# Routed experts in two-lane steps of 64 rows, in plain fp32, with rows added to the tokens by the transfers

## The chip, the cores and the metric

The kernel runs on one core of one Trainium2 chip. The metric is the device time of one execution in microseconds (us). Runs of the kernel before took 1578.53, 1578.96 and 1581.05 us, a median of 1578.96.

## What is computed

One layer of a decoder trunk for 1024 tokens of width 1024. The first half (a mixer of a convolution, a state-space branch and attention) is not touched. The second half is a mixture of experts with a layer norm behind it:

```
e_idx, e_w = grouped_top2_route(h2d, router_w, router_bias)      # 2 of 32 experts for each token
y = routed_experts(h2d, e_idx, e_w, w1, w3, w2)                  # (silu(x w1) * (x w3)) w2, by expert
y = y + swiglu(h2d, shared_w1, shared_w3, shared_w2)             # one shared expert
x = layer_norm(ALPHA * x + g2 * y, ln_g, ln_b)                   # ALPHA = 2 ** 0.25
```

1024 tokens with two experts each are 2048 rows, sorted by expert. An expert's weights are three pieces of 1 MB (1024 x 512 for the two up-projections side by side, in two pieces, and 256 x 1024 for the down-projection). With these inputs 23 of the 32 experts get rows.

## The kernel before

Rows of one expert are cut into blocks of 128 (BLK). There are 33 blocks here, and the loop's first stretch (STRETCH, line 42) runs 33 without asking. For each block `block` (line 1676) writes out the order of TensorE, ScalarE, VectorE and GpSimd by hand:

- `fetch` and `fetch_w` (from line 1595) load the weights of the block after next on SP's queue, each load under a condition that skips it if the expert in that buffer is already the right one. `ex_w` splits each weight piece into a rounded high half (ScalarE, line 125) and the rest (VectorE, line 129), both in the fp32r format.
- `ex_x` transposes the gathered 128 rows (8 transposes of 128 columns, line 1635), splits them in the same way, and `gather` (line 1610) has GpSimd issue an indirect transfer for the rows of block b + 2.
- `ex_up` multiplies with `mm3`: each product of 128 x 512 is three fp32r matmuls (lines 140 to 142). 8 products are the two up-projections.
- `ex_mid` transposes the hidden rows of block b - 1 (line 1654) and splits them; `ex_down` makes 4 products for that block, scales each row by its routing weight on ScalarE (line 1671), and GpSimd scatters the rows by an indirect transfer (line 1672) into `yd`. `yd` holds 2 x 1024 rows, one for each token and choice. Empty rows of a block have an index outside of the bounds and are left out.

A block so issues 36 matmuls of 512 columns and 10 transposes. The work of `ex_mid` and `ex_down` for a block stands one block later.

Ahead of the loop `shared_down` (line 1528) computes base = ALPHA * x + the shared expert (already times g2) for eight tiles of 128 tokens and keeps them in SBUF. `exp_start` (line 1562) issues the first conditional loads.

Behind the loop `final` (line 1706) loads g2 and the norm's two rows, spreads them over the partitions by matmuls (line 1719), loads both rows of each token (line 1729), adds them (for six of eight tiles by identity matmuls in plain fp32, line 1741), multiplies by g2, adds the base, and takes the layer norm: sum on VectorE, sum of squares on ScalarE (line 1753), scale and shift on ScalarE, GpSimd (line 1781) or VectorE (lines 1783, 1798), and the store on SP's queue (line 1784).

Another stage that the prediction reads is the state-space branch: at line 1013 it multiplies with tiles of 128 x 64, two side by side in TensorE's columns.

Of the kernel before, what the change touches and what calls it, by code (L numbers as in the profile page):

```python
# [39 lines left out]
SLOTS = {"wa": ["h2", "l2", "h3", "l3", 0, "x0"], "wb": [1, "h0", "l0", "h1", "l1", "x1"]}  # L40
PROLOGUE = ((0,), (0, 0), (0,), (0, 1), (0, 2), (0, 3), (1, 0), (0, 4))
STRETCH = (0, 33, 35, 39, MAXB)
# [38 lines left out]
class K:  # L81
# [86 lines left out]
    def build(self):  # L168
        with ExitStack() as ctx:
# [13 lines left out]
            self.x1d, self.h2d, self.yd = dt("x1d", [S, D]), dt("h2d", [S, D]), dt("yd", [2 * S, D])  # L183
# [33 lines left out]
            if self.stop in ("post", "shared"):  # L217
                return
            with ExitStack() as st:
                self.banks_for(tr=2, th=1, h=2, y=3)  # L220
                self.experts(pool(st, "exq"))
            est.close()
            with ExitStack() as st:
                self.banks_for(y=8)
                self.final(pool(st, "fin"))
# [12 lines left out]
    def pair(self, n, dt=F32R):  # L238


        if str(n)[0] == "x":
            return self.exp.tile([128, 2, D], dt, name=n, tag=n)
# [1146 lines left out]
    def ffn(self, wst):  # L1389
# [23 lines left out]
        self.wraw = [[self.pair(2 + 3 * z + q, F32) for q in range(3)] for z in range(2)]  # L1413
        for z in range(2):
            for q in range(3):
                nc.sync.dma_start(out=self.wraw[z][q][:].rearrange("p k n -> p (k n)"), in_=a["exp"][FIRST[z], q])
# [5 lines left out]
        with tc.manual_schedule(engines={mybir.EngineType.DVE}):  # L1422
            self.logits(P, 3)
            self.shared_up(w, hs, 0, 0)
            R.pick(6, 8)
            self.shared_up(w, hs, 0, 1)
            next(rows)
            self.shared_up(w, hs, 1, 0)
            self.shared_up(w, hs, 1, 1)
            g2 = self.shared_down(P, hs, rows)  # L1430
        wst.close()
        if self.stop == "shared":
# [3 lines left out]
            for i in range(NT):  # L1436
                self.dump(f"base{i}", self.base[i][:])
            return
        self.g2 = g2
# [88 lines left out]
    def shared_down(self, P, hs, rows):  # L1528
        nc, a = self.nc, self.a
        v = nc.vector  # L1530
        g2 = self.row_bc(P, "g2", self.adad[3:4, :])
# [12 lines left out]
        self.base = []  # L1544
        for i in range(NT):
            base = self.bslot(i)
            nc.sync.dma_start(out=base[:], in_=self.x1d[i * 128:(i + 1) * 128, :])
            self.base.append(base)
# [10 lines left out]
            self.ex_w(*PROLOGUE[i])  # L1559
        return g2  # L1560

    def exp_start(self):

        nc = self.nc
        self.turn = {"wa": 0, "wb": 0}
        self.ew, self.ex, self.eh = {}, {}, {}
        self.last_load = None
        self.nb = nc.values_load(self.be[0:1, 2 * MAXB:2 * MAXB + 1], min_val=0, max_val=MAXB)
# [5 lines left out]
    def experts(self, P):  # L1574
        tc, nc = self.tc, self.nc
# [6 lines left out]
        with ExitStack() as arms:  # L1582
            for b0, b1 in zip(STRETCH, STRETCH[1:]):
                if b0:
                    arms.enter_context(tc.If(self.nb > b0))
                    self.last_load = None
                with tc.manual_schedule(engines=MANUAL | {mybir.EngineType.Pool}):
                    self.ex_w(b0, 0)
                    self.ex_x(b0, 0)
                    self.ex_x(b0, 1)  # L1590
                    self.ex_w(b0, 1, 2, 3, 4)
# [3 lines left out]
    def fetch(self, b):  # L1595

        with ExitStack() as st:
            if self.last_load is not None:
                st.enter_context(self.tc.issue_after(self.last_load))
            self.fetch_reg(b)  # L1600
            for q in range(2):
                self.fetch_w(b, q)

    def fetch_reg(self, b):
        sync = self.nc.sync
        self.reg = (sync.value_load(self.be[0:1, b:b + 1], min_val=0, max_val=E - 1),
                    sync.value_load(self.be[0:1, MAXB + b:MAXB + b + 1], min_val=0, max_val=1))

# [5 lines left out]
    def fetch_w(self, b, q):  # L1614
        e, ld = self.reg
        d = self.nc.sync.dma_start(out=self.wraw[b % 2][q][:].rearrange("p k n -> p (k n)"), cond=ld,
                                   in_=self.a["exp"][bass.ds(e, 1), q].rearrange("z p n -> (z p) n"))
        self.last_load = d.ins

    def ex_w(self, b, *qs):  # L1620

        for q in qs:
            if (b, q) in self.ew:
                continue
            tg = "wa" if q < 4 else "wb"
            w = self.ew[b, q] = self.pair(SLOTS[tg][self.turn[tg] % len(SLOTS[tg])])
            self.turn[tg] += 1
            self.split_into(w[:, 0], w[:, 1], self.wraw[b % 2][q // 2][:, q % 2])

    def ex_x(self, b, n):  # L1630

        x = self.ex[b, n] = [self.exp.tile([128, 512], F32R, name="x" + z, tag="x" + z, bufs=2) for z in "hl"]
# [4 lines left out]
        self.split_into(x[0][:], x[1][:], ps[:])  # L1637
        if n and b + 2 < MAXB:
            self.gather(b + 2)

    def ex_up(self, b, ps, n):

        xh, xl = self.ex.pop((b, n))
        for k in range(4 * n, 4 * n + 4):
            w = self.ew[b, k // 2]
            xs, ws = slice((k % 4) * 128, (k % 4) * 128 + 128), slice((k % 2) * 512, (k % 2) * 512 + 512)
            self.mm3(ps[:], xh[:, xs], xl[:, xs], w[:, 0, ws], w[:, 1, ws], k == 0, k == KT - 1)

    def ex_mid(self, b):
# [5 lines left out]
        self.eh[b] = [self.exp.tile([128, 256], F32R, name="h" + z, tag="h" + z, bufs=1) for z in "hl"]  # L1655
        self.split_into(self.eh[b][0][:], self.eh[b][1][:], pt[:, :256])

    def ex_down(self, b):

        nc, P = self.nc, self.exp  # L1660
        hh, hl = self.eh.pop(b)
        w = [self.ew.pop((b, q)) for q in (4, 5)]
        y = P.tile([128, D], F32, name="y", tag="y", bufs=2)
        ps = [self.ps("y") for _ in range(2)]
        for k in range(2):
            ks = slice(k * 128, (k + 1) * 128)
            for n in range(2):
                sl = slice(n * 512, (n + 1) * 512)
                self.mm3(ps[n][:], hh[:, ks], hl[:, ks], w[k][:, 0, sl], w[k][:, 1, sl], k == 0, k == 1)
        for n in range(2):  # L1670
            nc.scalar.activation(out=y[:, n * 512:(n + 1) * 512], in_=ps[n][:], func=AF.Copy, scale=self.roww[:, b:b + 1])  # L1671
        nc.gpsimd.indirect_dma_start(out=self.yd[:], in_=y[:], in_offset=None,  # L1672
                                     out_offset=bass.IndirectOffsetOnAxis(ap=self.idx[:, 1, b:b + 1], axis=0),
                                     bounds_check=2 * S - 1, oob_is_err=False)

    def block(self, b, first, last):

        v, act = self.nc.vector, self.nc.scalar
        if b + 2 < MAXB:
            self.fetch(b + 2)  # L1680
        self.ex_w(b, 5)
        if b + 2 < MAXB:
            self.fetch_w(b + 2, 2)
        ps = self.ps("h")
        self.ex_up(b, ps, 0)
        if not first:
            self.ex_mid(b - 1)
        if not last:
            self.ex_w(b + 1, 0)
            self.ex_x(b + 1, 0)  # L1690
        self.ex_up(b, ps, 1)
        if not last:
            self.ex_x(b + 1, 1)
            self.ex_w(b + 1, 1, 2)
# [3 lines left out]
        if not last:  # L1698
            self.ex_w(b + 1, 3, 4)
        if not first:  # L1700
            self.ex_down(b - 1)
        if last:
            self.ex_mid(b)
            self.ex_down(b)

    def final(self, P):

        nc = self.nc
        v, act, gp, pe = nc.vector, nc.scalar, nc.gpsimd, nc.tensor
        ys = []  # L1710

        row = P.tile([128, 3, D], F32, name="frow")
# [391 lines left out]
```

## Time and profile before

| | |
|---|---|
| median of the timed runs | 1578.96 us |
| the profiled execution | 1582.0 us |
| its span, first to last instruction | 1579.9 us |
| TensorE busy | 1419.6 us (90%) |
| VectorE busy | 1196.8 us (76%) |
| ScalarE busy | 733.4 us (46%) |
| GpSimd busy | 442.5 us (28%) |
| mean granted clock of TensorE | 0.954 |
| moved by the DMA engines | 247.50 MB |

Everything in the trace is timed from the start of the span. In the trace PE is TensorE's matmuls, PEld its weight loads, DVE VectorE, ACT ScalarE, POOL GpSimd and SP the engine that issues most transfers. L1672 is line 1672 of the kernel. A matmul record's duration includes its way through the array, so the pitch of neighbouring records, not their duration, is what one costs. An indirect transfer on POOL shows the time that POOL takes to issue it; the chain of work and the waits tell when it landed.

### The profile page before, as it was taken

Reading aid. Unit: us, or ns where it says so; the run is one execution under the profiler, and the core shown is the slowest. Engines: PE = TensorE matmul, PEld = TensorE weight load, DVE = VectorE, ACT = ScalarE, POOL = GpSimd, SP = SyncE. Lnnn points to the kernel's source line nnn. Section 1 sums busy time; section 2 is a strip of 40 time slices with the busy share of each in tenths; the row PEclk is TensorE's granted clock in tenths of the full one; section 3 lists DMA queues with packets and bytes.
Section 4 is the critical chain, followed back from the end, with each engine's and each line's share of the span. In section 5 each row is a group of like instructions: output and inputs, shape, how many; then the busy total and the mean of one; then the engine's idle time right before and its main releaser. Section 6 shows DMA issues by size and latency. Waiting matters only on the chain.

```text
span 1579.9 us, 20183 instructions
## 1 busy us (share of the span) xinstructions
PE 1419.6 (90%) x6996; PEld 1144.4 (72%) x6996; DVE 1196.8 (76%) x1861; ACT 733.4 (46%) x1192; POOL 442.5 (28%) x599
## 2 busy tenths in 40 slices
PE   5599799479999999999799979999979999999983
PEld 3477678368888887887588867788967888888841
DVE  8464687898775547756587788778887999999948
ACT  6232112242223334130477763335424998999853
POOL 7999930000000000006211252400322322222216
PEclk9799999799999999999799998999999999999977
DMA  9232221132122248968200035634623777777643
GB/s 382 80 113 88 73 58 27 67 101 97 56 107 107 107 145 308 326 161 224 36 15 12 4 114 192 225 133 151 251 79 115 303 282 287 289 297 272 255 182 146
DMA packets 79940, 247.50 MB, mean 157 GB/s; under 512 B 18460, under 2 KB 29780, under 8 KB 71000
## 3 DMA queue, kind: packets, MB, share of 16 engines
q1 hardware_dynamic: 53670, 200.47, 36.0%
q10 hardware_dynamic: 15218, 24.68, 4.5%
q0 software_dynamic: 10944, 20.99, 4.2%
q8 instruction: 56, 0.92, 0.2%
q14 instruction: 52, 0.43, 0.1%
HBM read 252.74 MB, written 55.10 MB: 195 GB/s over the span
## 4 chain that ended last, share of the span: by engine, by line
PE 58%; DVE 14%; POOL 12%; DMA 7%; issue 5%; ACT 3%; ACTq 0%; DVEq 0%; POOLq 0%; SPq 0%
PE ps_mm L140 9%; PE ps_mm L141 9%; PE ps_mm L142 9%; DMA yd<-y,idx 4%; PE ps_up L140 3%; PE ps_h L140 3%; PE ps_h L142 3%; PE ps_h L141 3%; PE ps_up L141 3%; PE ps_up L142 3%; PE ps_O L1272 2%; PE ps_T L1258 2%; PE ps_y L140 1%; PE ps_y L142 1%; PE ps_tr L1635 1%
## 5 line engine op out<-in xcount | busy, mean ns | idle before, releaser
L1138 POOL TENSOR_TENSOR mg<-mg,sg 128x512 f32<-128x512 f32 x16 | 23.5, 1476 | 496.4 <-DVE sg L1137 492.8
L140 PE MATMUL ps_mm<-hh,wlo 128*128 128x512 f32 x304 | 123.5, 406 | 22.7 <-ACT sg L1075 15.6
L142 PE MATMUL ps_mm<-hh,whi 128*128 128x512 f32 x304 | 123.1, 405 | 0.0
L141 PE MATMUL ps_mm<-hl,whi 128*128 128x512 f32 x304 | 122.7, 404 | 0.0
L125 ACT CAST whi<-raw 128x1024 fp32r<-128x1024 f32 (+1 forms) x45 | 46.8, 1040 | 134.0 <-PE ps_up L142 65.2
L1672 POOL DMA_INDIRECT yd<-y,idx x33 | 46.5, 1409 | 170.4 <-ACT y L1671 98.4
L140 PEld LDWEIGHTS ps_mm<-hh,wlo 128*128 128x128 f32 x304 | 58.7, 193 | 37.6 <-ACT sg L1075 16.1
L129 DVE TENSOR_TENSOR qh<-wo,qh 128x1024 fp32r<-128x1024 f32 x66 | 80.5, 1220 | 5.1 <-ACT qh L125 5.1
L129 DVE TENSOR_TENSOR ql<-wo,ql 128x1024 fp32r<-128x1024 f32 x66 | 79.5, 1219 | 4.8 <-ACT ql L125 4.8
L129 DVE TENSOR_TENSOR wlo<-raw,whi 128x1024 fp32r<-128x1024 f32 x44 | 60.4, 1373 | 26.5 <-ACT whi L125 26.5
L125 ACT CAST qh<-wo 128x1024 fp32r<-128x1024 f32 x66 | 70.0, 1061 | 4.1 <-DMA wo<-exp 4.1
L142 PEld LDWEIGHTS ps_mm<-hh,whi 128*128 128x128 f32 x304 | 58.6, 193 | 14.9 <-issue 1.0
L141 PEld LDWEIGHTS ps_mm<-hl,whi 128*128 128x128 f32 x304 | 58.8, 193 | 13.7 <-issue 0.2
L125 ACT CAST ql<-wo 128x1024 fp32r<-128x1024 f32 x66 | 68.2, 1052 | 0.0
L125 ACT CAST xh<-ps_tr 128x512 fp32r<-128x512 f32 x66 | 39.5, 599 | 55.5 <-PE ps_tr L1635 55.4
L1610 POOL DMA_INDIRECT xg<-h2d,idx x35 | 37.1, 1061 | 77.1 <-PE ps_tr L1635 63.5
L1244 DVE TENSOR_REDUCE sm<-ps_S 128x1 f32<-128x256 f32 (+3 forms) x64 | 49.2, 770 | 10.8 <-PE ps_S L1241 10.1
L129 DVE TENSOR_TENSOR pl<-ps_T,ph 128x512 fp32r<-128x512 f32 (+1 forms) x80 | 45.9, 581 | 14.0 <-ACT ph L125 12.6
L140 PE MATMUL ps_up<-ah,wlo 128*128 128x512 f32 x128 | 50.6, 403 | 5.1 <-ACT ah L125 2.9
L391 DVE TENSOR_TENSOR sp<-ps_mm,sp 128x512 f32<-128x512 f32 x48 | 32.8, 686 | 28.0 <-PE ps_mm L142 27.8
L1245 ACT ACTIVATE p<-ps_S,sm 128x256 f32<-128x256 f32 (+3 forms) x64 | 48.5, 758 | 10.0 <-DVE sm L1244 9.4
L140 PE MATMUL ps_mm<-wo,ml 128*128 128x512 f32 x128 | 50.0, 398 | 2.8 <-DVE sg L1354 2.8
(727 smaller groups left out, 4733.2 us busy)
## 6 DMA issues: line engine op xcount, KB each, us to landing
wo<-exp SPq DMA_DIRECT2D x111, 1024.0 KB
raw<-w_in SPq DMA_DIRECT2D x43, 512.0 KB
adr<-w_ada SPq DMA_DIRECT2D x32, 512.0 KB
wada<-w_ada SPq DMA_DIRECT2D x16, 512.0 KB
fy<-yd SPq DMA_DIRECT2D x16, 512.0 KB
sga<-sg ACTq DMA_DIRECT2D x8, 512.0 KB
sgc<-sg ACTq DMA_DIRECT2D x8, 512.0 KB
sgs<-sg ACTq DMA_DIRECT2D x8, 512.0 KB
```

Of the source, the lines that this page charges most:

```text
L125: nc.scalar.copy(out=hi, in_=src)
L129: e.tensor_tensor(out=lo, in0=src, in1=hi.bitcast(F32), op=ALU.subtract)
L140: mm(ps, wl, xh, start=first, stop=False)
L141: mm(ps, wh, xl, start=False, stop=False)
L142: mm(ps, wh, xh, start=False, stop=last)
L391: v.tensor_tensor(out=out, in0=p, in1=x, op=op)
L1244: v.tensor_reduce(out=sm[:], in_=x, axis=AX.XY if two else AX.X, op=ALU.max, negate=True)
L1245: act.activation(out=y, in_=x, func=AF.Exp, bias=sm[:], accum_out=d)
L1258: pe.transpose(pt[:, k2 * 256 + qi * 128:k2 * 256 + qi * 128 + 128], prob[h, c, qi][:, ks], self.ident[:])
L1272: pe.matmul(po[:, 0:256], vv[:, kt, h].rearrange("p z d -> p (z d)"), x[z], start=kt == 0 and z == 0, stop=kt == 2 * c + 1 and z == 1)
L1610: self.nc.gpsimd.indirect_dma_start(out=self.xg[b % 2][:], out_offset=None, in_=self.h2d[:], in_offset=bass.IndirectOffsetOnAxis(ap=self.i ...
L1672: nc.gpsimd.indirect_dma_start(out=self.yd[:], in_=y[:], in_offset=None, out_offset=bass.IndirectOffsetOnAxis(ap=self.idx[:, 1, b:b + 1], ...
```

## The change

Blocks hold 64 rows. Two blocks are worked on at once, as a step: the first in lane 0 (columns 0 to 63 of TensorE, partitions 0 to 63 of the result), the second in lane 1 (64 to 127). Blocks are dealt to steps so that the lanes have their own experts, and each lane has its own two sets of raw weight buffers. 47 blocks of these inputs make 24 steps, and the loop's first stretch is now 24 steps. The weights, rows and hidden rows are used as plain fp32; there are no splits in the loop. The gated and weighted rows are added to `yd`, which now holds one row for each token and starts as the base, by two indirect transfers for each step, one a lane. The last norm reads one row for each token, and runs on ScalarE and VectorE alone.

```diff
-BLK = 128
+BLK = 64
+MAXS = (MAXB + 1) // 2
-STRETCH = (0, 33, 35, 39, MAXB)
+SLOTS = ((2, 3, 4), ("h2", "l2", "h3")), ((5, 6, 7), ("l3", 0, 1))
+STRETCH = (0, 24, 25, 27, MAXS)
...
+            nc.scalar.dma_start(out=self.yd[i * 128:(i + 1) * 128, :], in_=base[:])
...
     def fetch_w(self, b, q):
+            for z in range(2):
+                e, ld = self.regs[b][z]
+                d = self.nc.sync.dma_start(out=self.wx[z, b % 2][q][:].rearrange("p k n -> p (k n)"), cond=ld,
+                                           in_=self.a["exp"][bass.ds(e, 1), q].rearrange("z p n -> (z p) n"))
...
     def ex_x(self, b, n):
-        self.split_into(x[0][:], x[1][:], ps[:])
+        self.nc.scalar.copy(out=self.ex[b][:, n * 512:(n + 1) * 512], in_=ps[:])
+    def mm2(self, ps, x, w, first, last):
+        for z in range(2):
+            self.nc.tensor.matmul(ps[z * 64:(z + 1) * 64, :], x[:, z * 64:(z + 1) * 64], w[z], start=first, stop=last,
+                                  tile_position=(0, 64 * z))
     def ex_up(self, b, ps, n):
         for k in range(4 * n, 4 * n + 4):
+            self.mm2(ps, self.ex[b][:, k * 128:(k + 1) * 128],
+                     [self.wx[z, b % 2][k // 4][:, k // 2 % 2, ws] for z in range(2)], k == 0, k == KT - 1)
     def ex_mid(self, b):
+        self.nc.vector.tensor_copy(out=self.eh[b][:], in_=pt[:, :256])
     def ex_down(self, b):
         y = P.tile([128, D], F32, name="y", tag="y", bufs=2)
+        for n in range(2):
+            ps, sl = self.ps("y"), slice(n * 512, (n + 1) * 512)
+            for k in range(2):
+                self.mm2(ps, ht[:, k * 128:(k + 1) * 128], [self.wx[z, b % 2][2][:, k, sl] for z in range(2)], k == 0, k == 1)
+            nc.vector.scalar_tensor_tensor(out=y[:, sl], in0=ps[:], scalar=self.roww[:, b:b + 1], in1=self.g2[:, sl],
+                                           op0=ALU.mult, op1=ALU.mult)
+        for z in range(2):
+            nc.gpsimd.indirect_dma_start(out=self.yd[:], in_=y[:], in_offset=None,
+                                         out_offset=bass.IndirectOffsetOnAxis(ap=self.idx[:, 1 + z, b:b + 1], axis=0),
+                                         bounds_check=S - 1, oob_is_err=False, compute_op=ALU.add)
     def block(self, b, first, last):
         self.ex_up(b, ps, 0)
+            self.fetch_reg(b + 2)
+            self.fetch_w(b + 2, 0)
             self.ex_mid(b - 1)
             self.ex_x(b + 1, 0)
         self.ex_up(b, ps, 1)
+            self.fetch_w(b + 2, 1)
             self.ex_x(b + 1, 1)
             self.ex_down(b - 1)
+                self.fetch_w(b + 1, 2)
...
     def final(self, P):
+            nc.sync.dma_start(out=r[i][:], in_=self.yd[i * 128:(i + 1) * 128, :])
+        def stats(i):
+            act.activation(out=junk[:], in_=r[i][:], func=AF.Identity, accum_out=c(0, i))
+            act.mul(out=c(2, i), in_=c(0, i), mul=-1.0 / D)
+            act.activation(out=junk[:], in_=r[i][:], func=AF.Square, bias=c(2, i), accum_out=c(3, i))
+            act.activation(out=c(3, i), in_=c(3, i), func=AF.Identity, scale=1.0 / D, bias=eps[:])
             act.activation(out=c(4, i), in_=c(3, i), func=AF.Sqrt)
         def norm(i):
+            v.scalar_tensor_tensor(out=r[i][:], in0=r[i][:], scalar=c(2, i), in1=self.lg[:], op0=ALU.add, op1=ALU.mult)
...
+            v.scalar_tensor_tensor(out=r[i][:], in0=r[i][:], scalar=c(4, i), in1=self.lb[:], op0=ALU.mult, op1=ALU.add)
+            nc.sync.dma_start(out=self.out[i * 128:(i + 1) * 128, :], in_=r[i][:])
```

The transposes stay full-width (128 x 128). The router's index work is changed to blocks of 64 and to an index list for each lane; the two rows of the last norm are loaded ahead of the loop on ScalarE's queue (`last_rows`).

## Rows read from the trace of the kernel before

**Rows 1.** Busy time by stretch: us, busy (x instructions) by engine, clock, DMA share, GB/s.
```profile
1165.00:1204.00 39.00, 30.20 (x154) 24.16 (x152) 32.98 (x60) 8.32 (x10) 12.36 (x8) 0.91 0.14 46
1204.00:1516.00 312.00, 308.62 (x1510) 254.84 (x1510) 285.01 (x324) 273.67 (x389) 79.27 (x65) 1.00 0.71 264
1516.00:1580.00 64.00, 33.69 (x60) 13.71 (x60) 45.71 (x69) 27.33 (x61) 30.27 (x11) 0.71 0.50 199
```

**Rows 2.** The chain that ended last, from 1100: start us, us, what.
```profile
1204.14 0.50 PE ps_h L140
...
1402.87 0.44 PE ps_tr L1635 x4
...
1412.21 0.44 PE ps_tr L1635 x4
...
1440.59 8.06 DMA yd<-y,idx
...
1522.44 4.39 DMA fy<-yd
```

**Rows 3.** Timeline of PE in the last norm: start us, us, what.
```profile
1537.64 14.32 PE L1741 MATMUL ps_y<-fy,ident 128*128 128x512 f32 x33
```

**Rows 4.** Timeline of PE in the state-space stage.
```profile
130.59 0.33 PE L982 MATMUL ps_ss<-ident,kt 128*128 128x128 f32 x1
130.84 1.75 PE L1013 MATMUL ps_ss<-U,W 128*64 128x128 f32 x28
```

**Rows 5.** Groups from 1140 on, by form: busy us, mean ns | idle before, releasers.
```profile
L1672 POOL DMA_INDIRECT yd<-y,idx x33 | 46.5, 1409 | 170.4 <-ACT y L1671 98.4 <-ACT hh L125 36.8 <-ACT qh L125 16.8
...
L125 ACT CAST xh<-ps_tr 128x512 fp32r<-128x512 f32 x66 | 39.5, 599 | 55.5 <-PE ps_tr L1635 55.4
L1610 POOL DMA_INDIRECT xg<-h2d,idx x35 | 37.1, 1061 | 77.1 <-PE ps_tr L1635 63.5 <-DVE hl L129 7.8 <-issue 5.8
...
L1555 DVE SCALAR_TENSOR_TENSOR b<-b,ps_mm 128x512 f32<-128x512 f32 x16 | 10.3, 678 | 0.8 <-PE ps_mm L142 0.8
```

**Rows 6.** Waits of POOL from 1190 to 1519: us in total, times, longest us.
```profile
POOL yd L1672 <- ACT y L1671: 98.4, 21, 4.8
```

**Rows 7.** Stretches cut at landings of scatters in the chain; the last one alone.
```profile
1431.94:1435.95 4.01, 4.01 (x22) 3.31 (x21) 3.92 (x5) 3.14 (x6) 2.03 (x2) 1.00 0.29 111
1440.59:1448.65 8.06, 8.06 (x38) 6.61 (x38) 7.60 (x10) 7.20 (x11) 2.33 (x2) 1.00 0.95 368
1459.23:1465.98 6.75, 6.75 (x33) 5.53 (x33) 6.29 (x8) 5.89 (x9) 2.33 (x2) 1.00 0.96 364
...
1487.18:1496.26 9.08, 9.08 (x47) 7.54 (x46) 8.61 (x11) 8.21 (x13) 2.34 (x2) 1.00 0.96 356
1516.71:1520.00 3.29, 0.00 (x0) 0.00 (x0) 0.06 (x1) 1.00 (x1) 0.98 (x1) 0.90 0.15 47
```

**Rows 8.** Timeline of POOL at the loop's end: [idle before, releaser].
```profile
1497.04 1.00 POOL L1672 DMA_INDIRECT yd<-y,idx  x1 [5.37 <-DMA yd<-y,idx]
...
1516.71 0.98 POOL L1672 DMA_INDIRECT yd<-y,idx  x1 [3.53 <-ACT y L1671]
```

**Rows 9.** Timeline of SP's queue behind the loop.
```profile
1522.04 13.96 SPq L1729 DMA_DIRECT2D fy<-yd  x16
```

**Rows 10.** Groups of the last norm, from 1521, by form.
```profile
L1741 PE MATMUL ps_y<-fy,ident 128*128 128x512 f32 x48 | 23.1, 646 | 0.9 <-DMA fy<-yd 0.9
...
L1753 ACT ACTIVATE junk<-fy,fst 128x1024 bf16<-128x1024 f32 x8 | 9.2, 1148 | 5.5 <-DVE fst L1749 5.3
...
L1783 DVE SCALAR_TENSOR_TENSOR fy<-fy,fst,lb 128x1024 f32<-128x1024 f32 x3 | 3.8, 1278 | 0.0
...
L1759 ACT ACTIVATE fst<-fst,feps 128x1 f32<-128x1 f32 x6 | 1.7, 286 | 0.1
L1760 ACT ACTIVATE fst<-fst 128x1 f32<-128x1 f32 x8 | 1.6, 196 | 2.9 <-DVE fst L1757 2.9
L1753 ACT ACTIVATION_READ_ACCUMULATOR junk<-fy,fst 128x1 f32 x8 | 1.5, 186 | 0.0
```

More of the change, by code (lines that the diff above doesn't have):

```diff
@@ L1614, in fetch_w @@
     def fetch_w(self, b, q):
[L1615 to L1628, printed above, removed]
+        with ExitStack() as st:
+            if self.last_load is not None:
+                st.enter_context(self.tc.issue_after(self.last_load))
+            for z in range(2):
+                e, ld = self.regs[b][z]
+                d = self.nc.sync.dma_start(out=self.wx[z, b % 2][q][:].rearrange("p k n -> p (k n)"), cond=ld,
+                                           in_=self.a["exp"][bass.ds(e, 1), q].rearrange("z p n -> (z p) n"))
+                self.last_load = d.ins
     def ex_x(self, b, n):
-        x = self.ex[b, n] = [self.exp.tile([128, 512], F32R, name="x" + z, tag="x" + z, bufs=2) for z in "hl"]
+        if n == 0:
+            self.ex[b] = self.exp.tile([128, D], F32, name="xt", tag="xt", bufs=2)
         ps = self.ps("tr")
@@ L1662, in ex_down @@
[L1662 removed]
+        ht = self.eh.pop(b)
         y = P.tile([128, D], F32, name="y", tag="y", bufs=2)
[L1664 to L1669, printed above, removed]
[L1670 to L1671 removed]
@@ L1704, in block, with last_rows @@
             self.ex_down(b)
+            if b + 2 < MAXS:
+                self.fetch_w(b + 2, 2)
+    def last_rows(self, P):
+        self.lg, self.lb = (P.tile([128, D], F32, name=n) for n in ("lg2", "lb2"))
+        for t, n in ((self.lg, "ln_g"), (self.lb, "ln_b")):
+            self.nc.scalar.dma_start(out=t[:], in_=self.a[n][1:2, :].partition_broadcast(128))
     def final(self, P):
         nc = self.nc
-        v, act, gp, pe = nc.vector, nc.scalar, nc.gpsimd, nc.tensor
-        ys = []
-        row = P.tile([128, 3, D], F32, name="frow")
-        for i, src in enumerate((self.adad[3:4, :], self.a["ln_g"][1:2, :], self.a["ln_b"][1:2, :])):
-            nc.sync.dma_start(out=row[0:1, i], in_=src)
-        g2, lg, lb = (P.tile([128, D], F32, name=n) for n in ("g2", "lg2", "lb2"))
-        for i, t in enumerate((g2, lg, lb)):
-            for n in range(2):
-                ps, sl = self.ps("y"), slice(n * 512, (n + 1) * 512)
-                pe.matmul(ps[:], self.ones[0:1, :], row[0:1, i, sl], start=True, stop=True)
-                act.copy(out=t[:, sl], in_=ps[:])
+        v, act = nc.vector, nc.scalar
         st = P.tile([128, 6, NT], F32, name="fst")
@@ L1777, in affine @@
-        def affine(i):
-            r = ys[i][0]
-            if i < LAST:
-                for e, row, op in zip(GL[i], (lg, lb), (ALU.mult, ALU.add)):
-                    (v if e == "v" else gp).tensor_tensor(out=r[:], in0=r[:], in1=row[:], op=op)
-            else:
-                v.scalar_tensor_tensor(out=r[:], in0=ys[i][1][:], scalar=c(4, i), in1=lb[:], op0=ALU.mult, op1=ALU.add)
-            nc.sync.dma_start(out=self.out[i * 128:(i + 1) * 128, :], in_=r[:])
-        GL = ('gg', 'gg', 'gg', 'gg', 'gg', 'vv', 'vv', 'vv')
@@ L1787, in final @@
-        LAST = LT
-        with ExitStack():
-            for j in range(NT + 2):
-                if j < NT:
-                    gated(j, 0)
-                    gated(j, 1)
-                if 0 < j < NT:
-                    root(j - 1)
-                if j < NT:
-                    total(j)
-                    if j >= LAST:
-                        v.scalar_tensor_tensor(out=ys[j][1][:], in0=ys[j][0][:], scalar=c(2, j), in1=lg[:], op0=ALU.add, op1=ALU.mult)
-                    if j == NT - 1:
-                        norm(j - 1)
-                        affine(j - 1)
-                        affine(j - 2)
-                        root(j)
-                        norm(j)
-                        affine(j)
-                        break
-                if j:
-                    norm(j - 1)
-                if j > 1:
-                    affine(j - 2)
+            v.tensor_tensor(out=c(4, i), in0=c(4, i), in1=c(5, i), op=ALU.mult)
@@ L1813 @@
+            v.scalar_tensor_tensor(out=r[i][:], in0=r[i][:], scalar=c(4, i), in1=self.lb[:], op0=ALU.mult, op1=ALU.add)
+            nc.sync.dma_start(out=self.out[i * 128:(i + 1) * 128, :], in_=r[i][:])
+        for i in range(NT + 1):
+            if i < NT:
+                stats(i)
+            if i:
+                norm(i - 1)
 class Route:
```

224 lines of the change are left out of this document (87 added, 137 removed).

## The prediction, made before the changed kernel was run

> **What bounds the kernel now.** I read the stretches first, then the chain of work that ended last, then single timelines. The stretches say what fills the part that changes: from 1204 to 1516 PE is busy 308.62 of 312.00 us at full granted clock, and VectorE (285.01) and ScalarE (273.67) run nearly as full beside it because they make the high and low halves of every weight [rows 1]. So this stretch, the loop over 33 blocks, is TensorE's: it waits for almost nothing. The same view shows PE at 33.69 of 64.00 us after 1516, where the last layer norm runs. The chain's entries give the loop's beat: the first up-projection starts at 1204.14, and the transposes of two neighbouring blocks start at 1402.87 and 1412.21, 9.34 us apart [rows 2]. 33 x 9.34 = 308.2 us, to 1512.3; the last scatter is issued at 1516.71 [rows 8] and landed 3.29 later, at 1520.0 [rows 7], 7.7 us after the loop.
>
> **TensorE after.** The inputs fix the routing: 2048 rows over 23 experts make 47 blocks of 64, so 24 steps, which is also the first stretch that runs unconditionally. A step issues 12 products over both lanes (8 up, 4 down) and 10 transposes. The trace has no 64-column fp32 product of 512, so I bound it. A full-width plain fp32 product: 33 records in 14.32 us, 0.434 each [rows 3], and two records to a product (the stage's 24 products show as 48 [rows 10]), so 0.868. If the two lanes run side by side a pair costs 0.868 too; if one after the other, 1.736. The nearest row is the state-space stage, which already uses 128x64 tiles: 28 records of 128 columns in 1.75 us [rows 4]. One after the other, a 128-column record at 0.109 (a quarter of 0.434) would give 28 x 0.109 = 3.05; side by side 14 x 0.109 = 1.53 and some lead and drain. So they share. The same rows price a change of tile shape: from 130.59 to 130.84 a full-width record takes 0.25 instead of 0.11, about 0.15 lost. A step changes four times between lanes and full-width transposes.
> Step: 12 x 0.868 = 10.4, transposes 10 x 0.11 (four in 0.44 [rows 2]) = 1.1, switches 4 x 0.15 = 0.6: 12.1 us, with bounds 11.4 (no switch cost) and 12.9 (switches at twice that, and a little waiting for the copies). 24 x 12.1 = 290 against 308.2: 18 us less.
> The Trainium skill, "TensorEngine Tiling (Array Packing)", section "Key Properties", says that changing the tiling mode drains TensorE. The trace agrees, with those 0.15 us; by the rule alone no figure follows.
>
> **Splits and evacuations.** All splits go. VectorE keeps two gated evacuations of y (0.678 each, priced by the same operation from PSUM in line 1555), the gate product and the copy of the transposed hidden rows (half a copy's 512 columns, about 0.4 each); ScalarE two copies of x (0.599) and a Silu (about 0.4) [rows 5]. That is 2.2 and 1.6 us of 12.1: both are off the path at no cost, and TensorE covers them. POOL's own part of a step is a gather (1.06) and two scatters (1.41 each) [rows 5], 3.9.
>
> **The adds: the new wait.** Before, a block's scatter starts when its y is ready: what POOL mostly waits for there is ACT's y, 98.4 us in 21 waits [rows 6]. The landing of the one before is what the scatter at 1497.04 waited for, 5.37 us [rows 8]. All scatters write one tensor, so each waits for the last one's landing. Now there are two to a step, and gathers stand behind them on POOL; the y buffers (two) and so VectorE's evacuation and TensorE's third y bank hang on them. With a landing time L and 0.75 from a landing to the next issue (landed at 1496.26 where a stretch of [rows 7] ends, issued at 1497.04 [rows 8]) a step can't be shorter than 2 x (L + 0.75).
> L is in the stretches cut at the landings that the chain names (its entry of 8.06 us [rows 2] is one of these): 3.29 alone, 4.01 at 111 GB/s, and 8.06, 6.75 and 9.08 at 356 to 368 GB/s [rows 7]. So L goes with what else is moving: 4.01 x 111 = 0.45 MB moved meanwhile, 6.75 x 364 = 2.46, 8.06 x 368 = 2.97, 9.08 x 356 = 3.23. Before, an expert's three loads of 1 MB are issued nearly together; now the three stand after up0, up1 and down, some 4 us apart, so about 1.0 MB and the scatter's own quarter meet a scatter. On the line between 0.45 MB and 2.46 MB, 1.25 MB gives 5.1. An add must also read the target. No row shows it: its bounds are nothing, and the part after POOL's issue in the landing alone once more, 3.29 - 0.98 = 2.3 [rows 7, 8]. I take 0.4, near the lower end, because a scatter now carries at most 64 rows and 43 on the average (2048 / 48) where blocks of before held 62 (2048 / 33). L = 5.5, and the floor is 2 x 6.25 = 12.5: a hair above TensorE's 12.1. Taken for all 24 steps the loop is 300 us, to 1504. From both sides: L = 3.3 leaves TensorE's 290; L = 9.08 gives 19.7 a step, 472.
> The routing gives 20 experts to load in the loop (21 before, over 33 blocks), 60 pieces of 1 MB: an expert, 3 MB, in 12.5 us is 240 GB/s, under the 264 that [rows 1] show. Steps with two (three of 24) need 6 MB, 16 us at 370 GB/s; buffers two steps deep absorb it, up to 3 x 4 = 12 us if they don't.
> Ahead of the loop, the six 1 MB loads of step 1 and the base rows' writes to yd are issued in the shared expert's stage, 46 GB/s and a DMA share of 0.14 [rows 1]: at no cost. If the last base's write were late, the first add waits, two steps later; TensorE doesn't. The writes and the two rows of the last norm are issued on ScalarE's queue: a write waits for its base (VectorE's line 1555), and the loop's first copies of x stand behind it, so the loop can't start before the last base; before, it started after that stage too. SP's queue holds in the loop only register reads and loads, each behind the product that frees its buffer, in the order of the steps; a late one holds up only later loads.
>
> **Tail and last norm.** After the loop the last hidden rows, their down product and y take 5 us, and four scatters stand one after the other instead of one: the pair of step 22 (2 x 4.0 alone) while y of 23 is made, then two more (2 x 4.0). 16 us from the loop's end to the last landing against 7.7: +8.3. Landed: 1504 + 16 = 1520, as before.
> Then the norm: first load issued 2.0 after the landing (1522.04 [rows 9] against 1520.0), 4.39 to data as the chain has it before [rows 2]. ScalarE per tile: two passes of 1.148 + 0.186, two small ones of 0.196 and one of 0.286 [rows 10] = 3.35, eight tiles 26.8. VectorE: two passes of 1.278 and about 0.7 of small ones, 3.3, beside it; after the last root 2.0 remain, and a store, taken like that first load, 4.4. Sum 2.0 + 4.4 + 26.8 + 2.0 + 4.4 = 39.6 against 1579.9 - 1520.0 = 59.9 now: -20.3. The 33.69 us of PE, POOL's passes and half of the loads go. Bounds 36 to 44: tile statistics could stall on VectorE's chain.
>
> **Sum.** 1579.9 - 8.2 (loop at 12.5) + 8.3 (tail) - 20.3 = 1559.7 in span. The profiled execution took 1582.0 as a whole, and its span is 0.9 above the median of the timed runs, 1578.96. I subtract that: 1559.
>
> **Rivals.**
> The queue of adds binds (slower). If the spread loads don't help and scatters land as these four beside transfers did, L = (4.01 + 8.06 + 6.75 + 9.08) / 4 = 7.0 [rows 7], a step is 2 x 7.7 = 15.4, and the end 1559 + 24 x 2.9 = 1629. It decides from a step of 13.35 (1559 + 24 x 0.85 = 1579), L = 5.9; a mix of long and short landings lies between. For it: no scatter beside transfers is short in these rows; against it: bursts of 3 MB are gone, and 43 rows are fewer than 62. Chance 0.27.
> The add doubles the transfer (slower). L = 5.1 + 2.3 = 7.4 gives 16.3 a step, 1559 + 24 x 3.8 = 1650. Chance 0.08; no row of an add speaks for or against. The Trainium skill, "Collectives: The Full Stack", section "The bandwidth ceiling: the fold count and why AG ≠ RS ≠ AR", states this kind of cost: an add in the transfer reads two sources over one ring and so moves half as much. No run before the change shows it.
> The lanes don't share (slower). The step is 24 x 0.868 + 1.7 = 22.5, the end 1559 + 24 x 10.0 = 1799. Against it [rows 4]. Chance 0.03.
> The adds hide wholly (faster): L up to 5.3, the step is TensorE's 12.1, or 11.4 without switches: 1549, 1533 at best. Chance 0.2.
> My forecast, a step between 12.1 and 13.2: 0.35. About break-even: 0.07.
>
> **How the numbers follow.** Forecast 1559. 0.2% (3 us) is about what a measurement of this kernel can tell from no change. Faster is the forecast and the adds that hide, 0.55; same 0.07; slower the three others, 0.38. The range leaves out the best end of the hidden case (0.05), the lanes that don't share (0.03), the doubled add (0.08) and a little of the first rival: 1538 to 1640. As cases of both signs hold most of it, the forecast's own range is 1549 to 1576.
>
> **What the profile after would show.** Step starts in the chain 12 to 13 us apart: the sum holds; 15 or more with POOL waiting for DMA yd at each scatter and TensorE's y products waiting for VectorE: the first rival. VectorE and ScalarE under 25% busy in the loop; records of a lane pair 0.43 apart, else the lanes don't share; the stage after the last landing 39 us long, else the norm was mis-sized. A wait of TensorE for the loads would prove me wrong on the buffers.

## The result, and the profile after

The changed kernel takes 1627.66 us (median of 4 runs, 1624.96 to 1632.39) where the kernel before, timed beside it, takes 1578.74. The ratio is 1.0312, with a 95% interval of 1.0281 to 1.0343: 3% slower. The forecast was 1559 and faster; the first rival, in which the queue of adds binds, had said 1629.

The page of the changed kernel: the span, the busy time of each engine, and the chain that ended last by engine and by line.

```profile
span 1630.6 us, 19389 instructions
...
PE 1386.4 (85%) x6810; PEld 986.5 (61%) x6810; DVE 935.7 (57%) x1618; ACT 484.7 (30%) x867; POOL 428.5 (26%) x595
...
DMA 12%; issue 10%; POOL 2%; ACT 1%; PE 1%; DVE 1%; SPq 0%; POOLq 0%; DVEq 0%; ACTq 0%
DMA yd<-y,idx 10%; POOL yd L1661 2%; DMA wo<-exp 1%; PE ps_h L1629 1%; ACT junk L1717 0%; ACT junk L1719 0%; DMA ql<-exp 0%; DMA b<-yd 0%; DVE b L1729 0%; SPq L1610 0%; DVE b L1724 0%; DVE y L1657 0%; ACT L1721 0%; DVEq L2042 0%; PE ps_tr L1620 0%
```

VectorE lost 261 us of work and ScalarE 249, and none of it is in the time. The chain no longer runs through TensorE: it is the landings of the transfers into yd, POOL's issue of them, and "issue", which in this chain is the stretch up to the landing of a step's first add.

The loop with its tail, and the last norm (us, then busy us and instructions of PE, PEld, DVE, ACT and POOL, granted clock, DMA share, GB/s, as in [rows 1], whose stretch of the loop leaves out the end of the tail):

```profile
1212.00:1594.00 382.00, 305.29 (x1384) 107.37 (x1384) 53.50 (x96) 35.95 (x73) 99.56 (x71) 0.90 0.67 212
1594.00:1631.00 37.00, 0.00 (x0) 0.00 (x0) 22.74 (x48) 22.32 (x57) 0.00 (x0) 0.50 0.59 227
```

PE is busy 305 of the 382 us of loop and tail; in the loop before it was busy 309 of 312. Landmarks of the chain (start us, us, what), as in [rows 2], and the first load of the last norm:

```profile
1212.24 5.87 PE ps_h L1629 x16
...
1236.12 1.64 POOL yd L1661
...
1246.77 9.63 DMA yd<-y,idx
...
1264.21 6.49 DMA yd<-y,idx
...
1559.93 33.86 DMA yd<-y,idx
1594.00 3.79 DMA b<-yd
```

With them the 50.7 us between the two spans (1630.6 - 1579.9) divide into three:

| | before | after | difference |
|---|---|---|---|
| start of the loop | 1204.14 | 1212.24 | +8.1 |
| loop and tail, to the first load of the last norm | 317.9 | 381.8 | +63.9 |
| from that load to the end | 57.9 | 36.6 | -21.3 |

Most of the later start had passed before the base rows. The last sum of the first half and the first sum into a base row (start us, us, what), before and then after:

```profile
1104.29 0.69 DVE L1467 SCALAR_TENSOR_TENSOR r<-r,ps_mm 128x512 f32<-128x512 f32 x1 [0.71 <-PE ps_mm L142]
...
1175.35 1.29 DVE L1555 SCALAR_TENSOR_TENSOR b<-b,ps_mm 128x512 f32<-128x512 f32 x2 [0.55 <-PE ps_mm L142]
```

```profile
1109.50 0.68 DVE L1463 SCALAR_TENSOR_TENSOR r<-r,ps_mm 128x512 f32<-128x512 f32 x1
...
1183.26 1.28 DVE L1549 SCALAR_TENSOR_TENSOR b<-b,ps_mm 128x512 f32<-128x512 f32 x2 [0.54 <-DVE rbb L1918]
```

Of the 8.1 us, 5.2 had passed by the end of the first half, which the change doesn't touch, and 7.9 before the first base row was made. In the traces of the edits below the first half ends between 1104.4 and 1108.3; why, no run shows. From the first base row to the loop it takes 28.8 us before and 29.0 after.

What POOL does in a step of the loop (start us, us, what, and in brackets how long it stood idle before and what ended that); [rows 8] has the two lines of before:

```profile
1442.46 1.58 POOL L1661 DMA_INDIRECT yd<-y,idx  x1 [2.55 <-DMA yd<-y,idx]
1448.99 1.55 POOL L1661 DMA_INDIRECT yd<-y,idx  x1 [4.94 <-DMA yd<-y,idx]
1450.84 1.07 POOL L1600 DMA_INDIRECT xg<-h2d,idx  x1 [0.30 <-issue]
1461.93 1.58 POOL L1661 DMA_INDIRECT yd<-y,idx  x1 [10.02 <-DMA yd<-y,idx]
1468.16 1.55 POOL L1661 DMA_INDIRECT yd<-y,idx  x1 [4.65 <-DMA yd<-y,idx]
1470.02 1.06 POOL L1600 DMA_INDIRECT xg<-h2d,idx  x1 [0.30 <-issue]
1473.51 1.58 POOL L1661 DMA_INDIRECT yd<-y,idx  x1 [2.43 <-DMA yd<-y,idx]
```

Add, wait for it to land, add, gather, wait for it to land. The waits of POOL, VectorE and TensorE in the loop tell how it spreads (waited for: us in total, times, longest us):

```profile
POOL yd L1661 <- DMA yd<-y,idx: 240.7, 45, 10.0
...
DVE y L1657 <- DMA yd<-y,idx: 103.4, 18, 12.4
...
PE ps_tr L1620 <- DMA xg<-h2d,idx: 43.1, 11, 8.5
```

45 of the 48 adds wait for the one before, where ACT's y held 21 of 33 scatters before [rows 6]. VectorE waits to write y until an older y has been read by its add. TensorE waits for gathered rows, since a gather stands on POOL behind adds that wait. The step, from the first add of step 1 (1257.13) to that of step 21 (1559.93), is 302.8 / 20 = 15.1 us.

### The profile page after: what moved, and what is told of

The parts are those of the page before. It is cut to its first block, busy times and chain, and to the rows that moved or that the text cites. A ratio compares the mean times of both kernels' runs of the same rounds, so it can differ in the third digit from the quotient of the medians.

```text
span 1630.6 us, 19389 instructions
## 1 busy us (share of the span) xinstructions
PE 1386.4 (85%) x6810; PEld 986.5 (61%) x6810; DVE 935.7 (57%) x1618; ACT 484.7 (30%) x867; POOL 428.5 (26%) x595
## 5 line engine op out<-in xcount | busy, mean ns | idle before, releaser
L1629 PE MATMUL ps_h<-wo,xt 128*64 128x512 f32 x480 | 142.2, 645 | 4.2 <-ACT xt L1622 4.2
L1661 POOL DMA_INDIRECT yd<-y,idx x48 | 75.2, 1567 | 254.8 <-DMA yd<-y,idx 240.7
L1622 ACT COPY xt<-ps_tr 128x512 f32<-128x512 f32 x48 | 28.0, 586 | 306.8 <-PE ps_tr L1620 283.1
L1684 DVE TENSOR_TENSOR hd<-ps_h,hd 128x256 f32<-128x256 f32 x24 | 10.2, 424 | 164.8 <-ACT hd L1683 164.8
L1657 DVE SCALAR_TENSOR_TENSOR y<-ps_y,roww,g 128x512 f32<-128x512 f32 x48 | 34.2, 746 | 117.9 <-DMA yd<-y,idx 103.4
L1629 PE MATMUL ps_y<-wo,ht 128*64 128x512 f32 x288 | 89.8, 607 | 0.0
L1629 PE MATMUL ps_h<-ql,xt 128*64 128x512 f32 x192 | 88.2, 603 | 0.0
L1629 PEld LDWEIGHTS ps_h<-wo,xt 128*64 128x64 f32 x480 | 41.3, 148 | 62.2 <-issue 57.7
L1620 PE MATMUL ps_tr<-ident,xg 128*128 128x128 f32 x192 | 32.8, 297 | 43.4 <-DMA xg<-h2d,idx 43.1
L1620 PEld LDWEIGHTS ps_tr<-ident,xg 128*128 128x128 f32 x192 | 22.2, 148 | 65.5 <-issue 63.7
L129 DVE TENSOR_TENSOR pl<-ps_T,ph 128x512 fp32r<-128x512 f32 (+1 forms) x80 | 45.9, 580 | 13.6 <-ACT ph L125 12.3
```

What stands on the lines that cost most here:

```text
L129: e.tensor_tensor(out=lo, in0=src, in1=hi.bitcast(F32), op=ALU.subtract)
L1620: self.nc.tensor.transpose(ps[:, k * 128:(k + 1) * 128], self.xg[b % 2][:, (4 * n + k) * 128:(4 * n + k + 1) * 128], self.ident[:])
L1622: self.nc.scalar.copy(out=self.ex[b][:, n * 512:(n + 1) * 512], in_=ps[:])
L1629: self.nc.tensor.matmul(ps[z * 64:(z + 1) * 64, :], x[:, z * 64:(z + 1) * 64], w[z], start=first, stop=last, tile_position=(0, 64 * z))
L1657: nc.vector.scalar_tensor_tensor(out=y[:, sl], in0=ps[:], scalar=self.roww[:, b:b + 1], in1=self.g2[:, sl], op0=ALU.mult, op1=ALU.mult)
```

## The experiments

All are edits of the changed kernel. Its step is 15.1 us; in the expectation of plain_scatter it stands as 14.1 (and as 14 in that of one_add), because I divided by 23 where the two adds are 21 steps apart. The verdicts hang on 12.0 to 12.5 against 13 and more, and are not touched by it, but the spans that I expected of plain_scatter and no_loads were reckoned from it and came out some 25 us too long. Steps below are all taken from the first add of step 1 to that of step 21.

| run | edit | median us | span of the profile | step us |
|---|---|---|---|---|
| the changed kernel | | 1627.66 | 1630.6 | 15.1 |
| plain_scatter | two transfers that overwrite | 1568.24 | 1566.5 | 12.5 |
| no_loads | no loads from step 2 on | 1563.00 | 1561.2 | 12.3 |
| two_targets | second lane adds into its own tensor | 1550.99 | 1546.4 | 12.0 |
| one_add | one add for both lanes | 1549.68 | 1548.2 | 12.0 |
| one_plain | one transfer, no add | 1557.58 | 1552.9 | 12.0 |
| base_on_sp | base written from SP's queue | 1627.93 | 1626.2 | 15.5 |
| one_add_sp | one add, and base from SP's queue | 1541.64 | 1539.9 | 12.0 |

plain_scatter, no_loads and base_on_sp were run once each; the kernel before took 1583.27 beside these three and one_add, 1583.94 beside the others, and 1578.74 beside the changed kernel, so medians of different groups compare only within some 5 us.

**plain_scatter.** The adds become plain writes.

```diff
-bounds_check=S - 1, oob_is_err=False, compute_op=ALU.add)
+bounds_check=S - 1, oob_is_err=False)
```

> The two transfers of a step overwrite rows instead of adding (the sum over a token's rows is left out). After the change a row's packet takes 0.33 us where a scattered row took 0.16, and the steps are 14.1 us apart ((1559.93 - 1236.12) / 23). Theory 'the add's second read is what makes the pair too long': packets back to 0.16, a pair of landings about 1.3 us shorter on its full lane and 0.7 on the other, so the step falls to TensorE's own 12.3 (three stretches of 3.6 and transposes) and the span from 1630.6 to about 1590. Rival 'two serial landings beside the loads, whatever they do': the step stays at 13.5 or more and the span over 1615.

Measured: the step falls to 12.5 (1252.54 to 1502.07 over 20 steps), the span to 1566.5. The first theory stands: with transfers that only write, the pair nearly fits. The span lies 24 under the expected 1590, for the reason given above. One 64-row write with nothing beside it, the only one issued between 1500 and 1505 (time that POOL takes, then the time to landing):

```profile
L1661 POOL DMA_INDIRECT yd<-y,idx x1: 997/997/997, 1502.1 to 1502.1; - x1
...
DMA to landing us min/median/max: 3.2/3.2/3.2
```

**no_loads.** The adds stay; the loads of later experts are skipped.

```diff
+v.memset(k.be[:, 2 * MAXS:4 * MAXS].rearrange("p (z s) -> p z s", z=2)[:, :, 2:], 0)
```

> All conditional loads from step 2 on are skipped, so later experts are computed with the wrong weights; the adds and their rows stay. At the loop's end, with no loads beside, the pairs were 6.36 + 6.89 and 4.78 + 5.49 us from issue to issue. Theory 'the landings are long because of the loads beside them': a step of one 64-row and one smaller add is 6.4 + 5.2 = 11.6 at most, under TensorE's 12.3, so the loop runs at 12.3 and the span is about 1588. Rival 'the adds alone are too long': step at 13 or more, span over 1605.

Measured: step 12.3 (1244.26 to 1490.46), span 1561.2, 27 under the expected 1588. So the loads, too, are needed for the stall: without them a pair of adds nearly fits. A 64-row add by itself, between 1401 and 1407:

```profile
L1661 POOL DMA_INDIRECT yd<-y,idx x1: 1581/1581/1581, 1401.1 to 1401.1; - x1
...
DMA to landing us min/median/max: 6.1/6.1/6.1
```

6.1 to land instead of 3.2, and 1.58 of POOL's time instead of 1.00: that is the price of the add alone. In packets: the 64 rows of this add hold the transfer engines for 0.45 us a row, those of the write above for 0.17 (the expectation of plain_scatter has 0.33 and 0.16). Neither run says that its own cause is the cause; each takes away enough of a sum that is 3 us a step over the limit.

**two_targets.** Same adds, same rows, same loads; in the loop only the wait between the lanes goes. The last norm has to read and add the second tensor.

```diff
+self.yd2 = dt("yd2", [S, D])
...
-nc.gpsimd.indirect_dma_start(out=self.yd[:], in_=y[:], in_offset=None,
+nc.gpsimd.indirect_dma_start(out=(self.yd, self.yd2)[z][:], in_=y[:], in_offset=None,
```

> Both adds of a step stay as they are, with their rows and their reads; only the second lane's goes to a tensor of its own (zeros at first), so that each add waits for the landing of the same lane's add of the step before and not for the other lane's. The last norm reads both tensors and adds them on VectorE, as in the run with one add (which took 42 us from its first load to the end). Theory 'what cost the time is that the two wait for each other': 12.0 a step like with one add, span about 1550 to 1556. Rival 'two adds a step are more than the transfer queue or POOL can carry beside the loads': steps of 13 to 14 again, span 1580 or more.

Measured: step 12.0 (1239.91 to 1479.96), span 1546.4, ratio to the kernel before 0.979 (0.9761 to 0.9818). POOL's waits in its loop:

```profile
POOL yd L1665 <- DVE y L1661: 81.2, 23, 7.2
...
POOL yd L1665 <- DMA yd<-y,idx: 1.2, 3, 0.5
```

240.7 us of waiting for landings have become 1.2. The landings themselves are not shorter: with two adds in flight they take 4.5/8.8/12.0 us (least, median, most). So it is not what the adds take that cost the time, but that each had to land before the next could start.

**one_add.** One transfer a step, into 2048 rows by token and choice, so that no two rows of a step meet. The index list and the last norm, which adds the two halves, change with it.

```diff
-        for z in range(2):
-            nc.gpsimd.indirect_dma_start(out=self.yd[:], in_=y[:], in_offset=None,
...
-                                         bounds_check=S - 1, oob_is_err=False, compute_op=ALU.add)
+        nc.gpsimd.indirect_dma_start(out=self.yd[:], in_=y[:], in_offset=None,
...
+                                     bounds_check=2 * S - 1, oob_is_err=False, compute_op=ALU.add)
```

> One add a step for both lanes: yd has 2048 rows again (by token and choice, the first half the base, the second half zeros written ahead of the loop), so no two rows of a step meet and one indirect transfer carries up to 128 rows; the last norm reads both halves and adds them on VectorE, which also makes the sum that ScalarE made. Theory 'the queue of serial landings sets the step': one landing of 6 to 11 us fits under 12.3, so the step is 12.3, the loop with its tail 30 to 40 us shorter than in the change; the last stage is bound by VectorE at 8 x 4.6 = 37 plus 13, some 50 instead of 37.8. Span 1630.6 - 45 + 12 = about 1598 less what the tail saves (10): 1585 to 1600. Rival 'TensorE's lanes or the loads are what takes 14 us': step unchanged, span about 1640.

Measured: step 12.0, median 1549.68, ratio 0.9781 (0.9755 to 0.9808), 37 us under the expected range. I had reckoned 45 us off the loop and its tail; the loop and its tail take 300.4 (1205.73 to the first load at 1506.12) instead of 381.8, so 81. The last stage takes 42.1 instead of 36.6, not 50. In the loop TensorE is the limit again; the stretch of the loop:

```profile
1205.00:1494.00 289.00, 287.43 (x1376) 102.98 (x1378) 54.84 (x94) 36.36 (x73) 60.51 (x46) 0.99 0.84 279
```

An add of both lanes (64 and 37 rows), the only one issued between 1481 and 1482 and with no load beside it, lands no later than one lane's:

```profile
DMA to landing us min/median/max: 6.0/6.0/6.0
```

**one_plain.** One transfer a step and no add at all; the base stays in SBUF and is added at the end.

```diff
-nc.scalar.dma_start(out=self.yd[i * 128:(i + 1) * 128, :], in_=base[:])
+self.base.append(base)
...
-bounds_check=S - 1, oob_is_err=False, compute_op=ALU.add)
...
+bounds_check=2 * S - 1, oob_is_err=False)
```

> No adds at all: one plain indirect transfer a step puts both lanes' rows into 2048 rows by token and choice, the base stays in SBUF and isn't written out, and the last norm adds base and both rows on VectorE, half of the first sums on GpSimd. Theory 'TensorE's 12.0 is the step's floor': steps of 12.0 as with one add. The last stage has one pass more: VectorE 8 x 1.28 = 10 us more, half of it on GpSimd, so 5 to 10 over the 42 of the run with one add; the start is up to 4 earlier as no writes stand on ScalarE's queue. Span 1548 to 1556. If adds also slow TensorE's step in a way not yet seen, the step falls below 12.0.

Measured: step 12.0, span 1552.9, median 1557.58, ratio 0.9835 (0.9816 to 0.9855). 12.0 is TensorE's own: taking the adds away from a step where they are hidden gives nothing. The last stage takes 53.7 (first load 1499.20), 11.6 more than with one add, a little over what I expected: VectorE's two norm passes took 1.53 each in this run, where GpSimd adds beside them, and 1.28 in the run with one add, and its own part of the extra adds 1.75 instead of 1.28.

**base_on_sp.** Only the queue of the eight writes changes.

```diff
-nc.scalar.dma_start(out=self.yd[i * 128:(i + 1) * 128, :], in_=base[:])
+nc.sync.dma_start(out=self.yd[i * 128:(i + 1) * 128, :], in_=base[:])
```

> The eight writes of the base rows go to SP's queue instead of ScalarE's; all else as in the change. Theory 'the writes hold up ScalarE's first copies of x': TensorE's first up-projection starts at about 1208 instead of 1212.2, and the span falls by 0 to 4 us, since the queue of adds starts with the first step. Rival 'the copies wait for the gathered rows or the transposes': start unchanged. If SP's loads of step 2 are held up instead, TensorE waits for a weight load in the first steps.

Measured: the loop starts at 1203.8, 8.4 before that of the changed kernel. Of this, 4.6 is not the writes' doing: the first sum into a base row, ahead of the first write, starts that much earlier already.

```profile
1178.64 1.28 DVE L1549 SCALAR_TENSOR_TENSOR b<-b,ps_mm 128x512 f32<-128x512 f32 x2 [0.53 <-PE ps_mm L142]
```

From there to the loop it is 25.2 us here and 29.0 in the changed kernel: 3.8 for the writes, close to the 4 that were expected. The other traces agree: 28.8 to 29.5 in the four with the writes on ScalarE's queue (plain_scatter, no_loads, one_add, two_targets), 25.2 in one_add_sp and in one_plain, which has no such writes.

What held up the loop can be read in the changed kernel, in an entry of the chain, in ScalarE's timeline and in TensorE's:

```profile
1189.28 21.01 DMA wo<-exp
```

```profile
1200.61 10.96 ACTq L1552 DMA_DIRECT2D yd<-b  x4
1211.61 1.07 ACT L1622 COPY xt<-ps_tr 128x512 f32<-128x512 f32 x2 [13.63 <-issue]
```

```profile
1212.24 5.87 PE L1629 MATMUL ps_h<-wo,xt 128*64 128x512 f32 x16 [4.22 <-ACT xt L1622]
```

The last four writes were issued one by one up to 1211.56. The chain puts the last two of them down to the landing of a 1 MB load that was issued at 1189.28 and took 21 us, while the loads of step 1 filled the transfers (DMA share 0.64 from 1165 to 1212; 0.14 before [rows 1]). The first copies of x stood behind the writes, and TensorE waited 4.2 us for them. That wait has a price of its own. The loop's first up-projection in the changed kernel, and then in this run:

```profile
1212.24:1218.10 5.86, 5.86 (x17) 1.67 (x17) 0.00 (x0) 0.44 (x1) 0.00 (x0) 0.62 0.86 350
```

```profile
1203.82:1207.47 3.65, 3.65 (x18) 1.12 (x18) 0.00 (x0) 0.59 (x1) 0.99 (x1) 1.00 1.02 419
```

The same 16 records take 5.87 us at a granted clock of 0.62 (a mean of the two levels, 1.2 and 2.4 GHz) instead of 3.65 at 1.00: 2.2 us more, so the writes cost 6.0 by the first add (52.9 us after the first sum, here 46.8).

The median is that of the changed kernel (1627.93, in a single run, against 1627.66), and from the first sum into a base row to the end the two traces take 447.6 and 447.3 us: with the queue of adds as the limit, the steps were 15.5, and the gain was given back on the way.

**one_add_sp.** Both.

> The run with one add, and the base rows' writes on SP's queue. With one add the step is TensorE's own 12.0, so what the writes hold up ahead of the loop counts in full: theory 'the writes on ScalarE's queue cost the wait before the first up-projection': it starts up to 4.1 us earlier after the transposes (TensorE's wait for xt in the run with one add), span 1544 to 1548. Rival 'SP's queue is then late with the loads of step 2': span 1548 or more.

Measured: 1541.64 (five runs, 1541.3 to 1545.06), ratio 0.9738 (0.9721 to 0.9756), better than expected. With TensorE as the limit the earlier start counts: the loop starts at 1199.3, 6.5 before that of one_add. Of this, 3.6 is the writes' (25.2 us from the first sum into a base row instead of 28.8), and the first add stands 5.9 earlier against that sum. This version beats both kernels.

```profile
1199.00:1500.00 301.00, 287.51 (x1387) 102.86 (x1385) 56.35 (x96) 35.87 (x72) 63.04 (x48) 0.98 0.83 279
```

## Why the prediction was wrong

**TensorE's step: right.** 12.1 was forecast; where nothing else binds it is 12.0, in four runs to 0.01. The lanes share the columns. Six records of the changed kernel's down product (start us, us, engine, line, what):

```profile
1449.65 0.64 PE L1629 MATMUL ps_y<-qh,ht 128*64 128x512 f32 x1
1449.66 0.64 PE L1629 MATMUL ps_y<-wo,ht 128*64 128x512 f32 x1
1450.13 0.59 PE L1629 MATMUL ps_y<-qh,ht 128*64 128x512 f32 x1
1450.14 0.59 PE L1629 MATMUL ps_y<-wo,ht 128*64 128x512 f32 x1
1450.56 0.59 PE L1629 MATMUL ps_y<-qh,ht 128*64 128x512 f32 x1
1450.57 0.59 PE L1629 MATMUL ps_y<-wo,ht 128*64 128x512 f32 x1
```

The two lanes' records start 0.01 us apart. The second pair starts 0.48 after the first, and each one after it 0.43 after the last, as long as one full-width record takes [rows 3]. The 0.6 us a step that I put for the four changes between lanes and full-width transposes fit what stands ahead of these records:

```profile
1445.48 3.65 PE L1629 MATMUL ps_h<-wo,xt 128*64 128x512 f32 x16
1449.07 0.66 PE L1620 MATMUL ps_tr<-ident,xg 128*128 128x128 f32 x4
```

Eight pairs take 3.59 to the transposes where 8 x 0.43 is 3.44, and the four transposes 0.58 to the next pair where they were put at 0.44: some 0.15 at each change. No run took the changes away.

**Splits and evacuations: right.** VectorE and ScalarE are at 14% and 9% in the loop.

**The adds: the step that failed.** The mechanism was named (each add waits for the landing of the last, two to a step, gathers and y buffers behind them), and so was the point from which it decides, L = 5.9. The size of L was wrong. I took 5.5; a step of 15.1 with 0.7 from a landing to the next issue (1461.24 to 1461.93 in the chain) means 7.5 - 0.7 = 6.8. This is two terms:
- The add itself was put at 0.4 with bounds of 0 and 2.3, on the reason that fewer rows travel. For 64 rows alone it is 6.1 - 3.2 = 2.9, above even the upper bound; beside the loads it is 1.3 (next point), three times what I took. Of it 0.6 is POOL's issue (1.58 against 1.00), which I had not thought to change.
- The landing beside loads was put at 5.1. The writes of plain_scatter landed after 5.6 in the median (1236 to 1500), the adds of base_on_sp after 6.9, those of no_loads after 6.1. So the add costs 1.3 beside the loads and the loads 0.8 beside the adds; alone the add cost 2.9. Why the prices are smaller together, no run shows.

What I had wrong in the second was less the line between two landings than what I read from it. Four writes of plain_scatter met 1.2 to 1.3 MB and landed after 4.3 to 5.6 us, where the line gives 5.1 (issued at 1289.11, 1315.71, 1361.52 and 1491.06). But the 41 writes of that stretch met 1.6 MB in the mean, not 1.25.

Fewer rows were worth something only in small adds. At the end of no_loads, with no load beside them, adds of 7 and 31 rows landed after 4.7 and 4.8 us, adds of 37 and 64 rows after 6.0 and 6.2; the 101 rows of both lanes in one_add landed after 6.0.

A chance of 0.55 for faster on a floor of 12.5 against TensorE's 12.1 and a break-even of 13.35 was too much: L had to stay within 0.4 us of the value taken, and its own bounds were 3.3 and 9.1. The first rival, which took L from the landings of the trace as they stood (7.0), gave 15.4 a step and 1629. That it came within 2 us of the measurement is in part luck: it left the add out (1.3) and put the landing beside loads 1.4 above that of plain_scatter, and its loop and tail (69.7 us more than before) were 6 too long, which the late start made up for.

**The rule on adds.** The Trainium skill, "Collectives: The Full Stack", section "The bandwidth ceiling: the fold count and why AG ≠ RS ≠ AR", says of ReduceScatter that its add needs two source reads on one ring, and so runs at about half the rate of a copy. The runs agree in size: the part of the landing after POOL's issue is 6.1 - 1.6 = 4.5 for the add and 3.2 - 1.0 = 2.2 for the write. The bytes that the trace counts for the 64 rows are the same in both, 0.26 MB. The rival built on that size, 7.4 and 1650, put 2.3 on top of the loads in full where the add cost 1.3 beside them, and so lay 22 us too high.

**Ahead of the loop: wrong, though not by the 8.1 us of the table.** The writes of the base were costed at nothing, with the argument that the loop's first copies can't start before the last base anyway. That is true, but the base was ready at 1207.3 and its last write went out at 1211.56. By base_on_sp this costs 3.8 us to the loop's start and 6.0 to the first add. I had read the DMA share of that stage before the change (0.14), not with the 6 MB of loads and 4 MB of base rows that the change adds to it. In the stretch from the first base row to the loop as much of other work fell away (28.8 us before, 29.0 after); the rest of the later start had passed before that stretch, most of it in the first half.

**Tail and last norm: the last norm right.** It fell by 21.3 against a forecast of 20.3. The tail was not: I had put 16 us from the loop's end, with four adds of 4.0. TensorE's last transposes for the loop start at 1554.20, and six adds (1559.93 to 1589.90, 4.8 to 6.9 apart) still stood in the queue; the first load of the norm is at 1594.0. It is the same queue as in the loop.

**The sum.** Forecast: 0 ahead, -8.2 for the loop, +8.3 tail, -20.3 norm. Measured: +8.1, +63.9 for loop and tail, -21.3. Of the 64, the queue of adds accounts for 61: from the first add of step 0 (1236.12) to that of step 21 (1559.93) 323.8 us passed where 21 steps of 12.5 make 262.5 (the first of them alone took 21.0).

**The clock.** Waits cost a little more than themselves. In the step shown above, TensorE waits 5.2 us for gathered rows; the stretch of full speed, the stall, and the two after it:

```profile
1441.00:1456.00 15.00, 15.00 (x74) 5.33 (x72) 2.26 (x4) 1.46 (x3) 4.20 (x3) 1.00 0.96 330
1456.00:1463.00 7.00, 1.80 (x10) 0.92 (x6) 1.68 (x3) 0.00 (x0) 1.07 (x1) 0.72 0.60 216
1463.00:1466.00 3.00, 3.00 (x10) 0.84 (x10) 0.06 (x1) 0.58 (x1) 0.51 (x1) 0.51 0.40 55
1466.00:1468.00 2.00, 2.00 (x12) 0.50 (x8) 0.00 (x0) 0.00 (x0) 0.00 (x0) 1.00 0.29 57
```

After the stall the granted clock is 0.51, the lower of its two levels (1.2 GHz), for some 3 us, and then full again. A record of one lane of each pair, from TensorE's timeline:

```profile
1463.32 1.12 PE L1629 MATMUL ps_h<-ql,xt 128*64 128x512 f32 x1
...
1464.23 1.06 PE L1629 MATMUL ps_h<-ql,xt 128*64 128x512 f32 x1
...
1465.93 0.59 PE L1629 MATMUL ps_h<-ql,xt 128*64 128x512 f32 x1
...
1466.36 0.59 PE L1629 MATMUL ps_h<-ql,xt 128*64 128x512 f32 x1
```

Pairs start 0.91 us apart at the lower level and 0.43 at full clock. In the loop this is off the path, since the adds set the step; ahead of it, where TensorE waited for the copies, it is the 2.2 us of base_on_sp, which count once TensorE is the limit.

## What to carry to other kernels

When a change puts two operations in a row that each wait for the other's landing, take the landing from the trace as it stands, at its usual and not its best length, and ask by how much it may grow before it passes the engine that binds. If that margin (0.4 us here) is smaller than the bounds of a price that no row shows, the sign is open. Transfers into one tensor wait for each other here even where their rows can't meet (before the change one scatter waited 5.37 us for the last, into rows of its own [rows 8]), so give concurrent writers tensors of their own, or join them into one transfer: either made 3% slower into 2% faster here, with the same products and one more pass in the last norm, and with the base on SP's queue it was 2.6%. And a transfer issued from an engine that also computes holds up that engine's work when transfers are busy, so it belongs on a queue whose engine has nothing to do next.

## What the runs showed of the hardware

- An indirect add of 64 rows of 4 KB takes 6.1 us to land (no_loads), a plain write 3.2 (plain_scatter), each alone; POOL spends 1.58 us on issuing the add and 1.00 on the write.
- Alone, adds of 7 and 31 rows landed after 4.7 and 4.8 us, of 37, 64 and 101 rows after 6.0 to 6.2 (no_loads, one_add).
- One add of both lanes landed in the same 6.0 us as an add of one lane, so joining two transfers was worth a whole landing when alone; beside the loads it landed after 9.0 in the median (one_add), an add of one lane after 6.9 (base_on_sp).
- Two adds in flight at once landed after 8.8 us in the median, and yet two a step fitted into 12.0 us (two_targets).
- Two 128x64 tiles with a moving side of 512 in plain fp32 run side by side, a pair of records in 0.43 us, as a full-width record does [rows 3].
- After a wait of 4.2 us TensorE ran 16 records in 5.87 us at a granted clock of 0.62; without the wait the same records took 3.65 at 1.00 (the changed kernel and base_on_sp).
